# Storing batch 0 early and batch 14 on its own copies in a batched transposed matmul

## The chip, the cores and the metric

The kernel runs on one core of a Trainium2 chip. The metric is the device time of one execution in microseconds (us). A profile of one execution gives the span of the core's work, about 1.7 us less than that time. PE is the matmul engine, DVE and ACT copy and cast, SP issues most transfers, and 16 DMA engines carry them. One batch of `a`, or one output, is 512 x 512 x 4 bytes = 1.05 MB; the loads of `b` and most stores carry two batches.

## The reference

```python
batch, m, k, n = 16, 512, 512, 512          # a: [16, 512, 512], b: [16, 512, 512], float32
def reference(a, b):
    return np.matmul(a.transpose(0, 2, 1), b.transpose(0, 2, 1)).astype(np.float32)
```

It reads 33.55 MB and writes 16.78 MB.

## The kernel before

SP loads `a` batch by batch and `b` in pairs. DVE casts `b` to bf16, PE turns it, DVE copies it back; ACT casts `a`. PE then makes each output in four groups of four matmuls (`MO` is 4, and the semaphore `summed` counts groups). DVE copies out the first two groups of a batch, ACT the last two. A store takes two batches from one of five output buffers. Cuts are marked `...`.

```python
LOADS = 4; PAIRS = 3; OUTS = 5; LAG = 3; TAIL = 3; H = B // 2
def store(eng, j, part=slice(0, 2)):
    eng.dma_start(out_v[2*j + part.start:2*j + part.stop]..., o_sb[j % OUTS][:, part],
    ).then_inc(o_out[j % OUTS] if j + OUTS < H else stored, 16)

def run_sp(sp):
    for i in range(B):
        ...                                   # every second time: the load of a pair of b
        if use:
            sp.wait_ge(summed, MO * (i - LOADS) + 1)              # a's buffer is free
        if i % 2 == 0 and i // 2 >= OUTS:
            sp.wait_ge(o_out[i // 2 % OUTS], 16 * (i // 2 // OUTS))  # output buffer is stored
        sp.dma_start(a_sb[s][:], a_v[i]).then_inc(a_in[s], 16)
    for j in range(H - TAIL, H - 1):          # batches 10-11 and 12-13
        sp.wait_ge(summed, MO * (2 * j + 2) + 3)
        store(sp, j)
    sp.wait_ge(summed, MO * (B - 1) + 3)
    store(sp, H - 1, slice(0, 1))             # batch 14
    sp.wait_ge(last_go, 3)
    store(sp, H - 1, slice(1, 2))             # batch 15

def run_act(act):
    cast_a(act, 0)
    for i in range(B - 1):
        cast_a(act, i + 1)
        copy_out(act, i, slice(2, 4), oa_go)
        j, odd = divmod(i - LAG, 2)
        if odd and 0 <= j < H - TAIL:
            store(act, j)                     # so j goes at i = 2j + 4, behind the cast of a[2j + 5]
    copy_out(act, B - 1, 2, last_go)
    copy_out(act, B - 1, 3, last_go)
```

Of the kernel before, what the change touches and what calls it, by code (L numbers as in the profile page):

```python
# [11 lines left out]
def kernel(  # L12
# [8 lines left out]
    B, K, M = a.shape  # L21
# [3 lines left out]
    MO = M // P  # L25
# [13 lines left out]
    LOADS = 4  # L39
    PAIRS = 3  # L40
    OUTS = 5
    LAG = 3
    TAIL = 3
    H = B // 2
    STORED = H - (H - OUTS) + 1

# [4 lines left out]
    with tc.tile_critical():  # L51
        sb = lambda name, shape, dt: ctx.enter_context(nc.sbuf_tensor(name, shape, dt))
        ps = lambda name, shape, dt: ctx.enter_context(nc.psum_tensor(name, shape, dt))
        sem = tc.alloc_semaphore
        a_sb = [sb(f"a_sb{s}", [P, KO, M], f32) for s in range(LOADS)]
        b_sb = [sb(f"b_sb{s}", [P, NR, K], f32) for s in range(PAIRS)]
        o_sb = [sb(f"o_sb{s}", [P, 2, MO, N], f32) for s in range(OUTS)]
        a_bf = [sb(f"a_bf{s}", [P, KO, M], cdt) for s in range(2)]
# [10 lines left out]
        b_in = [sem(f"b_in{s}") for s in range(PAIRS)]  # L69
        o_out = [sem(f"o_out{s}") for s in range(OUTS)]  # L70
        turned = sem("turned")
        summed = sem("summed")
        last_go = sem("last_go")
        id_go = sem("id_go")

        bc_go = sem("bc_go")
# [5 lines left out]
        def store(eng, j, part=slice(0, 2)):  # L82


            eng.dma_start(
                out_v[2 * j + part.start:2 * j + part.stop].rearrange("b p mo n -> p b mo n"),
                o_sb[j % OUTS][:, part],
# [5 lines that stand above are left out]
                for p in ([0] if i == 0 else [(i + 1) // 2] if i % 2 and i + 1 < B else []):  # L93
                    if p >= PAIRS:
                        sp.wait_ge(turned, p - PAIRS + 1)
                    sp.dma_start(b_sb[p % PAIRS][:], b_v[p]).then_inc(b_in[p % PAIRS], 16)
                s, use = i % LOADS, i // LOADS
                if use:
                    sp.wait_ge(summed, MO * (i - LOADS) + 1)
                if i % 2 == 0 and i // 2 >= OUTS:  # L100

                    sp.wait_ge(o_out[i // 2 % OUTS], 16 * (i // 2 // OUTS))
                sp.dma_start(a_sb[s][:], a_v[i]).then_inc(a_in[s], 16)

            for j in range(H - TAIL, H - 1):
                sp.wait_ge(summed, MO * (2 * j + 2) + 3)
                store(sp, j)
            sp.wait_ge(summed, MO * (B - 1) + 3)
            store(sp, H - 1, slice(0, 1))
            sp.wait_ge(last_go, 3)  # L110
            store(sp, H - 1, slice(1, 2))
            sp.reg_mov(all_stored, 16 * STORED)
# [16 lines left out]
        def cast_a(act, i):  # L129
            s = i % LOADS  # L130
            act.wait_ge(a_in[s], 16 * (i // LOADS + 1))
            act.copy(a_bf[i % 2][:], a_sb[s][:]).then_inc(ac_go, 1)  # L132

        def copy_out(eng, i, rm, go):

            q = rm if isinstance(rm, int) else rm.stop - 1
            eng.wait_ge(summed, MO * i + q + 1)
            copy = eng.copy if eng is nc.scalar else eng.tensor_copy
            h = q // 2
            p = rm - 2 * h if isinstance(rm, int) else slice(None)  # L140
            copy(o_sb[i // 2 % OUTS][:, i % 2, rm, :], o_ps[h][:, p, :]).then_inc(go, 1)  # L141
# [35 lines left out]
        def run_act(act):  # L177
            cast_a(act, 0)
            for i in range(B - 1):
                cast_a(act, i + 1)  # L180
                copy_out(act, i, slice(2, 4), oa_go)
                j, odd = divmod(i - LAG, 2)
                if odd and 0 <= j < H - TAIL:
                    store(act, j)
            copy_out(act, B - 1, 2, last_go)
            copy_out(act, B - 1, 3, last_go)

        def run_pe(pe):
# [41 lines left out]
            with pe.Fori(0, H) as _i:  # L230
# [6 lines left out]
                half(1, 1)  # L237

        run_sp(nc.sync)
        run_pool(nc.gpsimd)  # L240
        run_dve(nc.vector)
        run_act(nc.scalar)
        run_pe(nc.tensor)

# [32 lines left out]
```

## Time and profile before

| | before |
|---|---|
| time, median of 3 | 124.81 us (124.78 to 124.95) |
| span of the profiled execution | 123.1 us |
| busy: PE, DVE, ACT | 70%, 46%, 38% |
| moved over the span | 50.33 MB, mean 409 GB/s |
| first and last store issued | 40.28 and 116.5 us |

The lines themselves are shown and read in the prediction.

### The profile page before, as it was taken

Reading aid. Unit: us, or ns where it says so; the run is one execution under the profiler, and the core shown is the slowest. Engines: PE = TensorE matmul, PEld = TensorE weight load, DVE = VectorE, ACT = ScalarE, POOL = GpSimd, SP = SyncE. Lnnn points to the kernel's source line nnn. Section 1 sums busy time; section 2 is a strip of 40 time slices with the busy share of each in tenths; the row PEclk is TensorE's granted clock in tenths of the full one; section 3 lists DMA queues with packets and bytes.
Section 4 is the critical chain, followed back from the end, with each engine's and each line's share of the span. In section 5 each row is a group of like instructions: output and inputs, shape, how many; then the busy total and the mean of one; then the engine's idle time right before and its main releaser. Section 6 shows DMA issues by size and latency. Waiting matters only on the chain. (4 is left out here: it accounts for less than half of the span.)

```text
span 123.1 us, 1084 instructions
## 1 busy us (share of the span) xinstructions
PE 85.9 (70%) x400; PEld 49.6 (40%) x400; DVE 56.4 (46%) x48; ACT 46.8 (38%) x34; POOL 0.7 (1%) x6
## 2 busy tenths in 40 slices
PE   0007497997999799769932599965992679979600
PEld 0007354643754564436402336533550526447200
DVE  0025377469295665907049007780719306162100
ACT  4004209438617903276300860329230590740300
POOL 2000000000000000000000000000000000000000
PEclk9999999999999999999995558999999558999985
DMA  4999999999999999999999999999999999999993
GB/s 96 389 399 453 407 426 461 434 383 461 426 391 461 426 341 431 429 431 439 437 407 426 445 429 415 429 423 434 463 397 431 423 426 426 429 426 431 426 421 130
DMA packets 5648, 50.33 MB, mean 409 GB/s; under 512 B 528, under 2 KB 528, under 8 KB 528
## 3 DMA queue, kind: packets, MB, share of 16 engines
q1 hardware_dynamic: 4288, 39.85, 77.4%
q10 hardware_dynamic: 1360, 10.49, 20.1%
HBM read 33.55 MB, written 16.78 MB: 409 GB/s over the span
## 5 line engine op out<-in xcount | busy, mean ns | idle before, releaser
L215 PE MATMUL o_ps<-bt_sb,a_bf 128*128 128x512 bf16 x256 | 65.0, 402 | 7.8 <-PEq L190 7.3
L132 ACT CAST a_bf<-a_sb 128x2048 bf16<-128x2048 f32 x16 | 30.4, 1901 | 40.5 <-DMA a_sb<-in_a_dram 40.5
L215 PEld LDWEIGHTS o_ps<-bt_sb,a_bf 128*128 128x128 bf16 x256 | 28.5, 115 | 38.1 <-issue 15.7
L201 PE MATMUL bt_ps<-identity,b_bf 128*128 128x128 f32 x144 | 24.1, 322 | 22.2 <-PEq L190 22.2
L141 DVE COPY o_sb<-o_ps 128x1024 f32<-128x1024 f32 x16 | 19.6, 1224 | 36.5 <-PE o_ps L215 36.5
L201 PEld LDWEIGHTS bt_ps<-identity,b_bf 128*128 128x128 f32 x144 | 22.2, 212 | 27.6 <-issue 26.6
L149 DVE CAST b_bf<-b_sb 128x2048 bf16<-128x2048 f32 x16 | 19.5, 1222 | 18.5 <-DMA b_sb<-in_b_dram 18.5
L141 ACT COPY o_sb<-o_ps 128x1024 f32<-128x1024 f32 (+1 forms) x17 | 16.3, 962 | 28.2 <-PE o_ps L215 28.2
L158 DVE COPY bt_sb<-bt_ps 128x1024 f32<-128x1024 f32 x16 | 19.5, 1216 | 2.9 <-PE bt_ps L201 2.9
L132 ACT ACT_TABLE_LOAD x1 | 1.3, 1283 | 0.9 <-SPq L51 0.9
L119 POOL TENSOR_SCALAR_AFFINE_SELECT identity<-identity 128x128 f32<-128x128 f32 x1 | 0.3, 292 | 0.2 <-POOL identity L117 0.2
L117 POOL MEMSET identity<- 128x128 f32 x1 | 0.2, 204 | 0.7 <-SPq L51 0.7
L261 POOL MEMSET const-bfloat16-1.0<- 128x1 bf16 x1 | 0.1, 101 | 0.0
L261 POOL MEMSET const-uint8-127<- 128x1 uint8 x1 | 0.1, 101 | 0.0
L261 POOL MEMSET const-float32-0.0<- 128x1 f32 x1 | 0.1, 98 | 0.2 <-issue 0.2
L261 POOL MEMSET const-float32-1.0<- 128x1 f32 x1 | 0.1, 98 | 0.0
## 6 DMA issues: line engine op xcount, KB each, us to landing
b_sb<-in_b_dram SPq DMA_DIRECT2D x8, 2048.0 KB, 20.5
a_sb<-in_a_dram SPq DMA_DIRECT2D x16, 1024.0 KB, 17.4
out_dram<-o_sb ACTq DMA_DIRECT2D x5, 2048.0 KB, 15.2
out_dram<-o_sb SPq DMA_DIRECT2D x2, 2048.0 KB, 13.8
out_dram<-o_sb SPq DMA_DIRECT2D x2, 1024.0 KB, 5.1
```

What stands on the lines that cost most here:

```text
L117: pool.memset(identity[:], 0.0).then_inc(id_go, 1)
L119: pool.affine_select(out=identity[:], in_=identity[:], compare_op=mybir.AluOpType.not_equal, fill=1.0, base=0, pattern=[[-1, P]], channel_ ...
L132: act.copy(a_bf[i % 2][:], a_sb[s][:]).then_inc(ac_go, 1)
L141: copy(o_sb[i // 2 % OUTS][:, i % 2, rm, :], o_ps[h][:, p, :]).then_inc(go, 1)
L149: dve.tensor_copy(b_bf[:, r, :], b_sb[p % PAIRS][:, r, :]).then_inc(bc_go, n)
L158: dve.tensor_copy(bt_sb[g][:].rearrange("p j (ni r) -> p j ni r", r=NR), bt_ps[:].rearrange("p j r (g ni) -> p g j ni r", g=2)[:, g],).the ...
L201: last = pe.transpose(bt_ps[:, j, r, :], w[:, r, j, :], identity[:])
L215: last = pe.matmul(o_ps[h][:, q, :], a_r[:, rk, 2 * h + q, :], bt_h[:, rk // 2, rk % 2, :], start=(rk == 0), stop=(rk == KO - 1),)
L261: nc = _bacc.Bacc("TRN2", target_bir_lowering=False, num_devices=1)
```

## The change

The intent: let writing begin as soon as the first output exists, and release the store of batch 14 when its own output is copied, without waiting for matmuls of batch 15.

```diff
-                    sp.wait_ge(o_out[i // 2 % OUTS], 16 * (i // 2 // OUTS))
+                    sp.wait_ge(o_out[i // 2 % OUTS], 16 * (i // 2 // OUTS + (i // 2 % OUTS == 0)))
...
-            sp.wait_ge(summed, MO * (B - 1) + 3)
+            sp.wait_ge(summed, MO * (B - 1) + 1)
+            sp.wait_ge(half_go, 1)
             store(sp, H - 1, slice(0, 1))
...
                 copy_out(act, i, slice(2, 4), oa_go)
+                if i == 1:
+                    store(act, 0, slice(0, 1))
                 j, odd = divmod(i - LAG, 2)
                 if odd and 0 <= j < H - TAIL:
-                    store(act, j)
+                    store(act, j, slice(0 if j else 1, 2))
+            act.drain().then_inc(half_go, 1)
             copy_out(act, B - 1, 2, last_go)
```

The first line counts one store more before output buffer 0 is used again, because two stores now empty it. At the new store of batch 0, ACT has just waited for the last group of batch 1, and PE starts that batch's two halves only after DVE and ACT have copied those of batch 0. The old wait was safe because PE starts the third group of batch 15 only after ACT has emptied that half of the accumulators, that is after ACT's copy of batch 14. In its place stand the first group of batch 15 (which implies DVE's copy) and ACT's drain (its own copy). `half_go` is the new semaphore that the drain sets. I call the early store *part 1* and the new wait of batch 14 *part 2*.

More of the change, by code (lines that the diff above doesn't have):

```diff
@@ L73 @@
         last_go = sem("last_go")
+        half_go = sem("half_go")
         id_go = sem("id_go")
```

## The prediction

> **What bounds the kernel now.** I read the page first, its slices and its chain of waits, then the waits of the loading queue, then short windows around the first store and the end.
>
> ```profile
> PE 85.9 (70%) x400; PEld 49.6 (40%) x400; DVE 56.4 (46%) x48; ACT 46.8 (38%) x34; POOL 0.7 (1%) x6
> DMA  4999999999999999999999999999999999999993
> GB/s 96 389 399 453 407 426 461 434 383 461 426 391 461 426 341 431 429 431 439 437 407 426 445 429 415 429 423 434 463 397 431 423 426 426 429 426 431 426 421 130
> HBM read 33.55 MB, written 16.78 MB: 409 GB/s over the span
> ```
>
> No compute engine is busy over 70%, while the DMA digit is 9 in all slices but the first and the last. The transfers are the bound. Neighbouring slices swing (383 then 461) because packets are counted where they fall, so I average over longer windows (start:end, length, busy time of PE, PEld, DVE, ACT, POOL, PE clock, DMA share, GB/s):
>
> ```profile
> 34.00:42.00 8.00, 7.06 (x36) 3.84 (x35) 6.61 (x6) 4.65 (x4) 0.00 (x0) 1.00 1.01 424
> 42.00:46.00 4.00, 4.00 (x24) 2.65 (x23) 1.83 (x2) 1.08 (x1) 0.00 (x0) 1.00 0.96 367
> 46.00:54.00 8.00, 6.03 (x29) 3.13 (x28) 5.16 (x5) 3.36 (x3) 0.00 (x0) 1.00 1.02 430
> ...
> 110.00:121.00 11.00, 5.80 (x32) 3.78 (x32) 1.23 (x1) 1.35 (x3) 0.00 (x0) 0.92 1.00 422
> ```
>
> Loads alone (34 to 42), loads beside stores (46 to 54) and stores alone (110 to 121) all run at 422 to 430, say 427 GB/s. The one dip, 367, falls just after the first store, which was issued at 40.28. The half-microsecond windows at the end show when the data stops:
>
> ```profile
> 120.50:121.00 0.50, 0.00 (x0) 0.00 (x0) 0.00 (x0) 0.00 (x0) 0.00 (x0) 0.50 0.86 360
> 121.00:121.50 0.50, 0.00 (x0) 0.00 (x0) 0.00 (x0) 0.00 (x0) 0.00 (x0) 0.50 0.09 33
> ```
>
> So the span adds up. 50.33 MB at 427 GB/s is 117.9 us. The first 4 us moved 33 and 246 GB/s in two windows of 2 us, 0.56 MB in place of 1.71, a loss of 2.7. The dip loses 4 x (1 - 367/427) = 0.6 at most. From the last data at 121.05 to the end at 123.1 are 2.0. Sum 123.2, against a span of 123.1. The time of a run is 1.7 more than the span (124.81).
>
> **What the Trainium skill says.** "DMA: Bandwidth & Descriptors", section "Where 436 GB/s comes from", gives 435 GB/s as the fabric ceiling and 425 as measured on a large transfer. The trace agrees with 422 to 430, so there is about 2% above the present rate and no schedule of mine raises it. The same page, section "Issuing engines are not separate DMA queues", says that transfers issued by different engines run on the same 16 DMA engines and interleave. The trace agrees: the rate is the same with one queue and with two. Its section "Queues, rings and completion order" says each DMA engine takes turns between queues packet by packet; I use this to share the bandwidth below. "TensorE: Matmul & The Clock Gate", part "The HAM clock gate", says that the matmul clock halves after an idle window of some 3.4 us. The trace shows clock 0.50 from 66 to 72 and from 96 to 102, after idle PE, so a load that comes late can slow the PE as well.
>
> **The change part by part.** It moves no bytes. One 2 MB store becomes two of 1 MB, one more issue of about 0.38 us on ACT's queue.
>
> *Part 1, batch 0 alone and early.* Today the first store is issued at 40.28. In the new kernel it goes behind the copy of batch 1, which ran at 25.87 for 1.02. So 1.05 MB of writing, 1.05/0.427 = 2.46 us of the DMA engines, enters among the loads some 13 us earlier. At that time the loads already keep the engines full, so it can't fill a gap; it delays what is queued behind it by up to 2.46 us. The store at 40 is 1 MB smaller, so the loads get the 2.46 us back there. What happens in between can be read from this stretch of ACT (start, length, what):
>
> ```profile
> 51.66 1.90 ACT L132 CAST a_bf<-a_sb 128x2048 bf16<-128x2048 f32 x1 [3.71 <-DMA a_sb<-in_a_dram]
> 51.67 0.38 ACTq L85 DMA_DIRECT2D out_dram<-o_sb  x1
> 53.47 1.00 ACT L141 COPY o_sb<-o_ps 128x1024 f32<-128x1024 f32 x1
> ```
>
> The later stores stand in ACT's program behind the cast of the next load, so each is released by a landing of a (51.66, 68.02, 82.24, 96.91). This makes the schedule correct itself: a load that lands late also holds back the next store, which then leaves the bandwidth to the loads. With half shares while both queues have work, I expect the loads between 30 and 45 us to land 2 to 3 late, the one at 51.66 some 1.2 to 1.7 late, the one at 68.02 some 1 early, and those from 82 on within 0.3 of now. The load of batch 10 waits today for the whole first store:
>
> ```profile
> SPq L102 <- DMA out_dram<-o_sb: 33.5, 3, 11.8
> ```
>
> It is issued at 54.73 after a store that took 14.4 from issue to landing. With half the store left, it should be issued near 51 to 52, and the longest wait (11.8) should fall to about 8 or 9. But six megabytes of older loads are still queued then, so it lands at about 70, as today. Worth to the end: 0.
>
> *Part 2, batch 14's store.* It waits today for the third group of batch 15 and is issued at 114.9. Afterwards it waits for the first group, two groups of four matmuls earlier (eight take 1.99), and for ACT's copy of batch 14, which ended at 110.2. The first group is done near 112, so it is issued 2 to 3 us earlier. Is there a gap that this fills? The times to landing of the last three stores, issued at 108.3, 114.9 and 116.5:
>
> ```profile
> DMA to landing us min/median/max: 8.9/8.9/8.9
> DMA to landing us min/median/max: 4.7/4.7/4.7
> DMA to landing us min/median/max: 5.6/5.6/5.6
> ```
>
> They land at 117.2, 119.6 and 122.1. That is 2.4 and 2.5 apart, the 2.46 us of 1 MB at full rate: they already lie back to back, and the window of 110 to 121 is full (1.00). An earlier issue only lengthens the queue. Gain 0. It does add slack: batch 14's data begins near 121.05 - 2 x 2.46 = 116.1, only 1.2 after the issue. The drain holds ACT alone, after its last-but-one copy, while ACT has several us to wait for PE (a wait of 4.76 in the trace): 0.
>
> Sum: 124.81 + 0 + 0, with the dip perhaps a little smaller since the first store is: 124.75.
>
> **The rivals.** *The dip goes away.* If it comes from how reads and writes meet at that place and not from the first store as such, the move could remove 0.4 to 0.6: 124.3. For it: later stores show no such dip. Against it: the first store remains and meets the same loads earlier, so I expect the dip to move to 28 to 34 us. *The compute chain becomes the end.* The last store is issued at 116.5 and its data begins near 121.05 - 2.46 = 118.6, so the chain from the last loads through PE has 2.1 us of slack, perhaps 1 of it taken by the latency of an issue. If part 1 delays the loads of batches 13 to 15, or moves PE's half clock from 95-102 to a place between 105 and 115, PE ends 2 to 4 later and the DMA runs dry for 1 to 3: 126 to 127.5. Against it: the schedule corrects itself by 82 us. *A gap exists that the windows hide.* Then part 2 would gain up to 0.5; the landings 2.4 and 2.5 apart speak against it.
>
> **Range and chances.** The two sums say no change. Downwards only the dip and some unevenness can go, 0.5 in all: 124.3. Upwards a little loss of bandwidth from one more store among the loads, or a small gap at the end: 125.2. A gain of over 2% would be 2.5 us, more than all losses that can be had (the 2.7 at the start are not touched): 1%. A loss of 2.5 needs the second rival in full: 3%.
>
> **What would show it.** Right: the DMA digits still 9 throughout; first store issued near 26; dip at 28 to 34; the casts of a released by loads late by 2 to 3 us around 38, and back at 82 and 97 within half a microsecond; batch 14's store issued near 112 with a longer time to landing (7 to 8); last landing near 122. Wrong: a DMA share below 0.97 in a stretch near the end, PE at half clock after 105, or a span under 122.6 with no dip at all.

## The result, and the profile after

| | before | after |
|---|---|---|
| median of 6 runs | 124.88 us (124.59 to 125.22) | 124.94 us (124.57 to 125.21) |
| ratio of fast runs | | 1.0001, 95% interval 0.9979 to 1.0024 |
| span of the profiled execution | 123.1 us | 123.1 us |

A ratio here and below is the mean time of one kernel's fast runs over that of the other's fast runs of the same rounds, so not quite the ratio of the medians quoted. The change moved nothing that can be told from noise; the interval leaves room for 0.3 us either way.

The slices of the page of the changed kernel, and its window 110 to 121 (columns as in the prediction):

```profile
DMA  4999999999999999999999999999999999999992
GB/s 91 378 407 455 407 426 461 426 391 461 389 418 423 453 402 423 431 463 421 407 426 426 466 410 413 429 426 439 434 413 431 429 423 426 431 429 426 429 418 101
...
110.00:121.00 11.00, 5.94 (x33) 3.79 (x32) 1.96 (x2) 2.19 (x3) 0.00 (x0) 1.00 0.99 415
```

The DMA engines are as full as before, from end to end (0.99 in this window, before 1.00). Inside this constant frame the transfers did move. ACT's casts start when a load of `a` lands, so the timeline of ACT shows the landings of batches 5, 9, 11 and 13. Before (batch 7, at 51.66, stands in the prediction):

```profile
38.16 1.90 ACT L132 CAST a_bf<-a_sb 128x2048 bf16<-128x2048 f32 x1 [0.74 <-DMA a_sb<-in_a_dram]
...
68.02 1.90 ACT L132 CAST a_bf<-a_sb 128x2048 bf16<-128x2048 f32 x1 [8.36 <-DMA a_sb<-in_a_dram]
...
82.24 1.90 ACT L132 CAST a_bf<-a_sb 128x2048 bf16<-128x2048 f32 x1 [4.12 <-DMA a_sb<-in_a_dram]
...
96.91 1.90 ACT L132 CAST a_bf<-a_sb 128x2048 bf16<-128x2048 f32 x1 [6.69 <-DMA a_sb<-in_a_dram]
```

After, with the new store and batch 7:

```profile
27.80 1.02 ACT L146 COPY o_sb<-o_ps 128x1024 f32<-128x1024 f32 x1 [3.65 <-PE o_ps L223]
27.81 0.40 ACTq L88 DMA_DIRECT2D out_dram<-o_sb  x1
...
40.94 1.90 ACT L137 CAST a_bf<-a_sb 128x2048 bf16<-128x2048 f32 x1 [1.58 <-DMA a_sb<-in_a_dram]
...
53.20 1.90 ACT L137 CAST a_bf<-a_sb 128x2048 bf16<-128x2048 f32 x1 [3.32 <-DMA a_sb<-in_a_dram]
...
67.61 1.90 ACT L137 CAST a_bf<-a_sb 128x2048 bf16<-128x2048 f32 x1 [6.41 <-DMA a_sb<-in_a_dram]
...
82.28 1.90 ACT L137 CAST a_bf<-a_sb 128x2048 bf16<-128x2048 f32 x1 [4.68 <-DMA a_sb<-in_a_dram]
...
96.95 1.90 ACT L137 CAST a_bf<-a_sb 128x2048 bf16<-128x2048 f32 x1 [5.12 <-DMA a_sb<-in_a_dram]
```

The early store made batch 5 land 2.8 us later and batch 7 1.5 later. Batch 9 came 0.4 earlier, and batches 11 and 13 within 0.04 of before: the delay was given back and nothing of it reached the end. The waits of SP for a store, in the window 40 to 56, before and then after (total, times, longest):

```profile
SPq L102 <- DMA out_dram<-o_sb: 11.1, 1, 11.1
```
```profile
SPq L105 <- DMA out_dram<-o_sb: 6.4, 1, 6.4
```

The load of batch 10 now waits 4.7 us less for its output buffer. This too is worth nothing: it was issued 2.7 us earlier and landed at 70.3, before at 70.2, with older loads queued ahead of it (that of batch 9 landed at 67.6). At the end, the times to landing of the three last stores of the changed kernel, issued at 109.3, 113.2 and 117.5:

```profile
DMA to landing us min/median/max: 7.8/7.8/7.8
DMA to landing us min/median/max: 6.4/6.4/6.4
DMA to landing us min/median/max: 4.6/4.6/4.6
```

They land at 117.1, 119.6 and 122.1, where the same three landed before at 117.2, 119.6 and 122.1. Batch 14's store went out 1.7 us earlier and landed at the same time. PE was about 1 us later in this execution (the last copy began at 116.85, before at 115.85), and so was the last store; this was still within the slack.

### The profile page after: what moved, and what is told of

Same layout as the page of the kernel before. It is cut to its first block, busy times and chain, and to the rows that moved or that the text cites. A ratio compares the mean times of both kernels' runs of the same rounds, so it can differ in the third digit from the quotient of the medians.

```text
span 123.1 us, 1087 instructions
## 1 busy us (share of the span) xinstructions
PE 88.6 (72%) x400; PEld 49.7 (40%) x400; DVE 56.6 (46%) x48; ACT 46.7 (38%) x34; POOL 0.7 (1%) x6
## 5 line engine op out<-in xcount | busy, mean ns | idle before, releaser
L223 PE MATMUL o_ps<-bt_sb,a_bf 128*128 128x512 bf16 x256 | 68.7, 420 | 9.8 <-PEq L198 9.4
L223 PEld LDWEIGHTS o_ps<-bt_sb,a_bf 128*128 128x128 bf16 x256 | 29.2, 117 | 42.3 <-issue 21.6
L209 PE MATMUL bt_ps<-identity,b_bf 128*128 128x128 f32 x144 | 23.3, 313 | 18.4 <-PEq L198 18.4
L209 PEld LDWEIGHTS bt_ps<-identity,b_bf 128*128 128x128 f32 x144 | 21.6, 211 | 24.3 <-issue 23.5
```

The source lines that it names most:

```text
L209: last = pe.transpose(bt_ps[:, j, r, :], w[:, r, j, :], identity[:])
L223: last = pe.matmul(o_ps[h][:, q, :], a_r[:, rk, 2 * h + q, :], bt_h[:, rk // 2, rk % 2, :], start=(rk == 0), stop=(rk == KO - 1),)
```

## The experiments

Twelve kernels were run in four calls, each beside the kernel before on the same chip, whose medians were 124.75, 124.95, 124.76 and 124.97 us (single runs 124.53 to 125.35). One-core runs more than 1.5% over the fastest of their kernel are called slow and left out of the ratios. This is a rule about times only: LAG 1's slow runs had granted clocks of 0.915 and 0.902, its fast ones 0.904 and 0.909. Where a kernel's own times spread (late14, LAG 1, LAG 2, LAG 5, lag4_a0act), the rule cuts the upper end, and the ratio may understate the loss. The medians are of all runs.

| run | edit | median us | ratio to before, 95% interval |
|---|---|---|---|
| p1_alone | part 1 only | 124.87 | 1.0010, 0.9986 to 1.0034 |
| p2_alone | part 2 only | 124.78 | 0.9998, 0.9976 to 1.0020 |
| late14 | batch 14 stored with batch 15 | 125.47 | 1.0049, 1.0003 to 1.0094 |
| no_store0 | after, batch 0 never stored | 122.50 | 0.9809, 0.9783 to 0.9834 |
| lag1 | before, LAG 1 | 129.94 | 1.0297, 1.0237 to 1.0358 |
| lag2 | before, LAG 2 | 125.51 | 1.0046, 0.9994 to 1.0097 |
| lag2_p2 | LAG 2 and part 2 | 126.47 | 1.0087, 1.0035 to 1.0139 |
| lag4 | before, LAG 4 | 124.75 | 0.9998, 0.9975 to 1.0020 |
| lag5 | before, LAG 5 | 129.50 | 1.0346, 1.0314 to 1.0377 |
| a0_act_b | before, first load of `a` by ACT | 124.73 | 0.9982, 0.9961 to 1.0003 |
| a0_act_a | after, first load of `a` by ACT | 124.97 | 1.0000, 0.9983 to 1.0018 |
| lag4_a0act | LAG 4, first load of `a` by ACT | 125.78 | 1.0079, 1.0035 to 1.0123 |

### Each part alone

The theory was that a queue without gaps makes the place of a store worthless. The rival was that the two parts hide each other: a loss by one, a gain by the other.

```diff
# p1_alone: the changed kernel with the old wait
-            sp.wait_ge(summed, MO * (B - 1) + 1)
-            sp.wait_ge(half_go, 1)
+            sp.wait_ge(summed, MO * (B - 1) + 3)
-            act.drain().then_inc(half_go, 1)
# p2_alone: the kernel before with the new wait
-            sp.wait_ge(summed, MO * (B - 1) + 3)
+            sp.wait_ge(summed, MO * (B - 1) + 1)
+            sp.wait_ge(half_go, 1)
+            act.drain().then_inc(half_go, 1)      # ACT, ahead of its last two copies
```

> Part 1 alone: batch 0 stored early, the tail waits as before. Theory T (the DMA engines carry 50.33 MB at 427 GB/s without a gap, so moving a store moves no time): 124.8 to 125.0, within 0.2 of the kernel before. Rival R1 (part 1 delays the compute chain, and part 2 pays that back): PE ends about 1 us later, batch 14's store is issued near 116 rather than 114.9, its data is wanted at 116.1, so the queue runs dry for 0.5 to 1.0: 125.4 to 125.9.

> Part 2 alone: batch 0 and 1 stored together as before, batch 14's store released by its own copies. Theory T: 124.8 to 125.0, the store is issued near 112 and lands at the same 119.6. Rival R2 (part 2 closes a gap at the end that part 1 opens again): 0.5 faster, 124.3.

Both are at 1.001 or nearer to 1, and the intervals exclude the rivals' half per cent of loss or gain. The premise of the first rival fell as well: with part 1 alone PE's last copy began at 116.05, near the 115.85 of before, and with part 2 alone at 116.95. So the later PE of the changed kernel is not part 1's doing. Both profiles with part 2 show it, but it arose before any instruction that part 2 adds had run, near 110: from 102 to 104 PE was at half clock in both (0.50), and eight matmuls that turn `b` took 1.91 us; before and with part 1 alone the clock there was 0.96 and 0.87, and they took 1.11. Why the clock came back later was not tested.

### Holding batch 14 back

```diff
# late14, on the kernel before
-            sp.wait_ge(summed, MO * (B - 1) + 3)
-            store(sp, H - 1, slice(0, 1))
             sp.wait_ge(last_go, 3)
+            store(sp, H - 1, slice(0, 1))
             store(sp, H - 1, slice(1, 2))
```

> The kernel before with the store of batch 14 held back to that of batch 15 (both after the last copy, issue near 116.5 and 116.9). Measures the slack at the end. Theory T: the data of the store before ends at 116.1, the held one's begins some 1 us after its issue at 116.5, so the engines stand idle 1.2 to 1.6: 126.0 to 126.5. Rival R3 (the end is not set by the queue): below 125.2.

This is part 2 turned the other way. Half-microsecond windows at the end of late14, the last two columns being DMA share and GB/s:

```profile
116.00:116.50 0.50, 0.00 (x0) 0.00 (x0) 0.00 (x0) 0.29 (x1) 0.00 (x0) 1.00 0.04 16
116.50:117.00 0.50, 0.00 (x0) 0.00 (x0) 0.00 (x0) 0.00 (x0) 0.00 (x0) 1.00 0.00 0
117.00:117.50 0.50, 0.00 (x0) 0.00 (x0) 0.00 (x0) 0.00 (x0) 0.00 (x0) 1.00 0.83 344
```

The queue was empty at 116, the store was issued at 116.3 and data flowed from about 117.0. So with the queue empty this issue took some 0.7 us to become traffic, and holding the store by 1.4 us left the engines idle for about 1.3 us (the shares above, and 0.48 from 115.5 to 116). The loss, 0.5% or 0.6 us in the mean of the fast runs and 0.8 us in that of all six, was about half of what I had expected (126.0 to 126.5), and its interval starts just above no loss. The median lies between theory T and rival R3 (below 125.2), and the runs spread from 124.52 to 126.39, over both. That the varying end of PE shows in the time once the slack is gone would explain the spread; one profile does not show it. In the profile before, the old release at 114.9 was early enough; part 2 makes it earlier still, on the flat side of this step.

### Taking bytes away

```diff
# no_store0, on the changed kernel (wrong on purpose: batch 0 stays unwritten)
-                if i == 1:
-                    store(act, 0, slice(0, 1))
# and the wait of o_out back to 16 * (i // 2 // OUTS)
```

> The changed kernel without the store of batch 0 (its output is not written: wrong on purpose), 1.05 MB less. Theory T: all bytes count, 1.05 MB at 427 GB/s less, 2.46 us: 122.3 to 122.6. Rival R4 (the chain of loads, PE and last store has no more than 1 or 2 us of slack and takes over): 123.0 to 124.0. If an early store were free (hidden): 124.9.

If the early store were hidden, leaving it out would save nothing. It saved 1.9%, 0.0191 x 124.8 = 2.4 us, against 1.05/0.427 = 2.46 for its bytes. PE was no second limit: it ended earlier too, with the last copy beginning at 113.35, because every later load came earlier. So the store costs its full bandwidth where it stands among the loads. Moving it saves nothing because something else then waits for those 2.46 us, as the landings above show.

### Moving all stores

The theory so far said that the place of a store is free. LAG sets how many batches behind a store is issued, so one digit moves all five of ACT's stores.

```diff
-    LAG = 3
+    LAG = 1      # lag1; lag2, lag4 and lag5 alike
```

> The kernel before with every ACT store two batches earlier (LAG 1 in place of 3): part 1's idea for all stores. Theory T (the queue is never dry, so the place of a store is free): 124.7 to 125.1, loads around 30 to 45 us up to 5 us late, back in step later. Rival R5 (early stores starve PE of loads, PE ends later than the 2 us of slack): 126 or more. Rival R6 (early stores even out the traffic and gain): 124.3 or less.

> The kernel before with every ACT store two batches later (LAG 5). Theory T: place is free only while the queue has work. Here the loads reach batch 9 near 58 us, batch 10's load must wait for the first store, which now lands near 62 or later, so the queue runs dry for 1 to 3 us after 58: 126 to 128, with DMA digits below 9 in the middle. If the place of a store did not matter at all: 124.9.

LAG 1 refuted the theory in this general form, as rival R5 had it. The windows of its profiled execution (a slow run of its kernel, 130.53; its fast runs were 127.79 and 129.57, so sizes are not to be taken from here):

```profile
106.00:110.00 4.00, 4.00 (x15) 2.47 (x14) 1.41 (x2) 0.98 (x1) 0.00 (x0) 0.50 1.01 426
110.00:116.00 6.00, 5.56 (x24) 2.53 (x22) 3.26 (x3) 3.22 (x3) 0.00 (x0) 0.97 0.31 131
...
119.00:123.00 4.00, 3.21 (x18) 1.94 (x16) 1.23 (x1) 1.17 (x2) 0.00 (x0) 1.00 0.63 262
```

The DMA engines are full up to 110, then less than a third busy (0.31) while PE works nearly all the time, full again from 116 to 119 (0.97, not shown), then short of work again (0.63). Batch 13 was cast at 102.30 here, against 96.91 before, and of the 6.4 us by which PE's last copy began later (122.25 against 115.85), these 5.4 were the larger part: stores that are always two batches ahead keep 2 x 2.46 = 4.9 us of transfers ahead of the loads. Nothing pays this back. At the end there is then no store left to carry while PE makes the last batches. The queue of stores that the old kernel leaves for the end is what covers PE's last chain.

LAG 5 failed as expected, but by more (129.5 in place of 126 to 128). In its profile (again a slow run, 132.46) the rate falls to 102 GB/s in the window 62 to 66: SP had waited 17.6 us, until 62.8, for the first store, issued only at 52.44, before it could load batch 10. The rate fell again twice (341 GB/s from 81 to 86, 216 from 98 to 101).

```profile
62.00:66.00 4.00, 3.12 (x18) 1.87 (x17) 2.68 (x3) 1.01 (x1) 0.00 (x0) 1.00 0.43 102
```

The revised theory was that a store's place is free as long as the queue is dry neither in the middle (stores too late, buffers not free) nor at the end (stores too early). Half steps were to test it.

> All ACT stores one batch earlier (LAG 2). Revised theory T2: the place of one store in the middle is free, but at the end the stores still queued must cover PE's work after the last loads; two batches earlier for all (LAG 1) let the loads of a land 5 us later and the queue ran dry 5 us. Half the step delays them by 2 to 3, of which 1 us is slack: 126.0 to 126.8, with the DMA share below 0.9 somewhere after 110. Rival R7 (LAG 1 was slow for another cause, such as more contention or the half clock alone): DMA share 1.0 to the end, 124.7 to 125.3.

> LAG 2 with part 2. T2: where the queue runs dry at the end, batch 14's store is worth its earlier issue: it goes out 2 to 3 us earlier into an idle queue, so 0.3 to 1.2 faster than LAG 2 alone: 125.2 to 126.2. If part 2 is worth nothing even with a dry queue: as LAG 2.

> All ACT stores one batch later (LAG 4). T2: more stores are left for the end, so none dry there; but the load of batch 10 waits for a first store that now lands near 60, just as the loads before it run out near 61: 0 to 1 us dry in the middle, 124.8 to 126. LAG 3 is then the best of the five.

LAG 2 falls into two groups: fast runs of 124.51, 124.66 and 124.83, and of 126.19 and 126.27; a sixth, 127.34, counts as slow. Its median lies below the range I gave. LAG 2 with part 2 does the same (124.91, 125.04 and four of 126.44 to 126.74). The profiles happened to catch one of each. LAG 2, a run of 124.66:

```profile
110.00:113.00 3.00, 2.93 (x19) 2.04 (x18) 0.98 (x1) 0.00 (x0) 0.00 (x0) 1.00 1.03 437
```

LAG 2 with part 2, a fast run of 126.44:

```profile
110.00:113.00 3.00, 2.42 (x11) 1.01 (x9) 2.36 (x2) 2.18 (x2) 0.00 (x0) 1.00 0.50 210
113.00:118.00 5.00, 4.64 (x27) 3.45 (x29) 1.22 (x1) 0.47 (x1) 0.00 (x0) 1.00 1.01 419
118.00:121.00 3.00, 1.07 (x5) 0.34 (x3) 0.00 (x0) 1.17 (x2) 0.00 (x0) 1.00 0.83 344
```

The slower group is the one with the dry queue, at half rate from 110 to 113, and it is in the fast state, so this supports the revised theory where LAG 1 could be doubted. What decides between the groups is open. In the slow one batch 13 was cast at 99.17, and PE ran eight matmuls of it in 3.58 us; in the other it was cast at 97.12 and they took 1.99. That is a coincidence seen in one profile each. Whether part 2 helps where the queue does run dry is not settled either: LAG 2 with part 2 was no faster, and the share of the groups decides the means. In its trace the first gap comes ahead of the store of batches 12 and 13, which part 2 doesn't touch.

LAG 4 is as fast as LAG 3. In its profile PE's last copy began at 110.85, 5 us before the one of LAG 3, so it has more slack at the end for the same time.

### The start, and the dip after the first store

```diff
# a0_act_b on the kernel before, a0_act_a on the changed one
+            act.dma_start(a_sb[0][:], a_v[0]).then_inc(a_in[0], 16)      # ACT's first instruction
-                sp.dma_start(a_sb[s][:], a_v[i]).then_inc(a_in[s], 16)
+                if i:
+                    sp.dma_start(a_sb[s][:], a_v[i]).then_inc(a_in[s], 16)
```

> The kernel before with the first load of a issued by ACT at its start in place of SP, so both queues have work from about 1 us on. The largest loss is the start (the first 4 us move 0.56 MB in place of 1.71, 2.7 us). Theory S1 (one issuer's descriptors limit the start): the rate of 2 to 4 us rises from 246 to 330 or more GB/s, 0.4 to 0.8 us faster, 124.0 to 124.4. Theory S2 (each engine's first packets are slow whoever issues them): the same, 124.7 to 125.0. It also tests whether the dip at the first store is the first use of ACT's queue: then there is none here.

> The changed kernel with the first load of a issued by ACT, as in the run before this one. S1: 124.0 to 124.4. S2: 124.7 to 125.0.

The rate of 2 to 4 us rose from 246 and 229 GB/s to 274 and 287, less than the 330 asked for, while that of the first 2 us fell from 33 to 25 and 8, and the times agree with no change. A second issuer is not what the start lacks. The edit also had a cost: the first cast of `b` began at 11.28 and 11.43 in these two profiles, before at 8.61, so PE began 2.7 us later. The dip after the first store is not the first use of ACT's queue, for it is there in a0_act_a, where that queue had carried a load:

```profile
34.00:38.00 4.00, 3.12 (x19) 2.21 (x19) 1.82 (x2) 2.81 (x2) 0.00 (x0) 1.00 0.97 377
```

Its early store was issued at 30.3. After the same store in the changed kernel, issued at 27.81, no window of 4 us from 26 to 42 is below 412. In a0_act_b, whose first store was issued at 44.4, the window 46 to 50 has 406. And late14, whose first store is that of the kernel before with its 367, shows 412 in 42 to 46:

```profile
42.00:46.00 4.00, 4.00 (x24) 2.66 (x24) 1.82 (x2) 1.10 (x1) 0.00 (x0) 1.00 0.98 412
```

So the dip varies between executions of the same first store. Nor does it stand far out: before any store, the kernel before shows 395 GB/s from 24 to 28 and 399 from 32 to 36. Its cause stays open.

### The two best edits together

```diff
-    LAG = 3
+    LAG = 4
# and the first load of a by ACT, as above
```

> LAG 4 with the first load of a issued by ACT: the two single edits that looked best, together. In the profile of LAG 4 PE ends 5 us before it has to, so the end cannot be late; the load by ACT raised the rate of 2 to 4 us from about 245 to 280 GB/s, worth at most 0.2 us. If both add up: 124.4 to 124.7, with little spread. If the start varies by more than that from run to run: the same as the kernel before, 124.7 to 125.0, ratio within 0.998 to 1.002.

A miss: 0.8% slower than the kernel before. Its profile (a fast run, 125.91) shows the rate falling in the middle, where LAG 4 alone had 414 GB/s in the same window:

```profile
74.00:78.00 4.00, 4.00 (x12) 1.49 (x11) 0.76 (x1) 0.00 (x0) 0.00 (x0) 0.57 0.89 340
```

As in the two runs before, `b` came later at the start (first cast at 11.81, LAG 4 alone 8.81), PE began 3.0 us later, and ACT's first store was issued at 49.99 in place of 48.63. That this tipped a LAG 4 which stands at the other edge of what is free is the likely reading, but no run isolates it. No version beat both kernels clear of noise.

## Why the prediction was right

**The bound.** Full DMA engines at 427 GB/s in all mixes carried it. The proof is no_store0: 1.05 MB less, 2.4 us less.

**Part 1.** Expected: batches around 30 to 45 us late by 2 to 3, batch 7 by 1.2 to 1.7, batch 9 early by 1, batches from 82 us within 0.3. Measured: 2.8, 1.5, 0.4 early and 0.04. The first store went out at 27.81 and not near 26, since PE was later there in this execution. The load of batch 10 was expected near 51 to 52 and came at 52.0; but I had taken the longest wait, 11.8, for the wait of that load. It was that of batch 12's load, and the longest stayed at 11.5; batch 10's own was 11.1 and fell to 6.4, so the "8 or 9" was worked from the wrong wait. The "six megabytes" of older loads were four to five (batches 8 and 9 of `a`, a pair of `b` and the rest of batch 7).

The half shares are the weakest step. The packet times of ACT's queue, which the packed traces hold and no view prints, show that the first store before, issued at 40.28, moved from 44.1 to 54.0 at 211 GB/s, and the early store of the changed kernel, issued at 27.81, from 31.3 to 38.0 at 158. While they move, half of 427 is right for the one and too much for the other; but both began only 3.5 to 3.8 us after their issue, a delay behind queued loads that the prediction did not have. The lateness of the loads came out right all the same. An estimate from the bytes of stores that these packets show ahead of each load gives 2.5 us for batch 5 and 1.2 for batch 7, whatever the shares.

On the clock, the quoted idle window of 3.4 us is longer than what the profile before shows: PE's matmuls ended at 93.05, and the clock fell near 95.3 (0.83 from 94 to 96 is full clock for 1.3 of 2 us), an estimate of 2.3 us.

**Why it corrects itself.** The step is right for one store and was too general as I put it. The later stores hang on landings of `a`, so the order after batch 7 is that of before. But a change that advances all stores shifts that order itself, and then it doesn't come back (lag1, 3% slower).

**Part 2.** Expected: issue near 112, 7 to 8 us to landing, gain 0. Measured: 113.2 and 6.4, with PE 1 us later, and the same landing at 119.6. The drain ended 1.9 us before the issue and cost nothing, as expected. Alone it gave 0.9998. The slack was sized well: 1.2 us for batch 14, of which an issue into the empty queue of late14 took 0.7, and holding the store by 1.4 us made the engines idle.

**The dip.** It could not be predicted from one profile. I expected it to follow the first store to 28 to 34 us. The changed kernel shows 412 GB/s from 30 to 34, about 4 x (1 - 412/427) = 0.14 us, but other executions with the same store show more, and with the old place less. It is part of the noise of half a microsecond that the range held.

**The rivals.** None came about. In the profile of the changed kernel the dip was nearly gone, as the first asks, but without its gain of 0.4 to 0.6. Of the signs of being wrong, the half clock came near: it lasted to about 104.9 (0.77 from 104 to 106), with 105 as the limit. The compute chain did become the end in lag1 and in the slower half of LAG 2, as the second rival described, though by moving every store.

## What to carry to other kernels

Where the DMA engines are full from start to end, an earlier store only takes its bandwidth from a load: ask what gets it back, and when, before expecting a gain. A queue of finished stores left for the end is a reserve that hides the last compute, and moving stores forward spends it; moving them back spends the free buffers. Try the setting one step to each side to see where the flat part ends before adding edits that look free.

## What the Trainium skill lacked or had wrong

- "DMA: Bandwidth & Descriptors", section "Bandwidth", has its 425 GB/s for loads issued by GpSimd. The trace adds that loads issued by SP, stores issued by SP, and loads beside stores issued by ACT all run at 422 to 430 GB/s on one core, with no loss from mixing directions.
- "Perfetto Trace Analysis", section "What 'DMA-bound' means", names what may bind but nothing of the order of loads and stores. The runs show that the same bytes cost 3% more when all stores go two batches earlier, and 3.5% more when two batches later.
- No page says how the rate of a program's first transfers builds up: the first two windows of 2 us moved 33 and 246 GB/s, and a second issuing engine raised the latter only to 274 to 287, with 25 and 8 in the first.
- No page has the delay of a store behind another queue's loads: 3.5 to 3.8 us from issue to first packet in the two profiles above, against 0.7 with the queue empty.
- No page has the dip after a first store: 367 GB/s over 4 us in one execution and 412 in another with the same first store (loads alone vary down to 395).
